# Fused SSD + latent-attention layer on one core: 64-row tiles padded, the y half of the out-projection ahead of its norm, one-bank PSUM tiles, another issue order up to the FFN

## The chip, the cores and the metric

The kernel runs on one core of a Trainium2 chip. The metric is the device time of one execution in microseconds (us), lower is better. The five engines of the core are named as the profile names them: PE (matrix multiply, with PEld for its weight loads), DVE (vector), ACT (scalar, activations), POOL (GpSimd, which also issues some DMAs) and SP (which issues most DMAs).

## The reference, cut to what matters

One layer of a hybrid encoder for 576 tokens at once, 512 of a new stream (the prompt) and 64 of a running stream (the sample), all in float32:

```
h   = rmsnorm(x, norm_mix) @ w_in            # z | xBC | dt | q latent | kv latent + rope key
xBC = silu(causal_conv(xBC))                 # 8 tiles of 128 channels
y   = ssd_scan(x, dt, A, B, C, state)        # chunked linear recurrence, 8 heads of 64
y   = rmsnorm((y + D*x) * silu(z), ssd_norm) # one factor per token, over 512 channels
o   = mla_attend(q, ckv cache + new, rope)   # 8 heads, block-causal softmax
x2  = x + concat(y, o) @ w_out               # out-projection: y half and o half
x3  = x2 + (silu(n@w_gate) * (n@w_up)) @ w_down,  n = rmsnorm(x2, norm_ffn)   # d_ff 2816
out = rmsnorm(x3, norm_final)
```

## The kernel before, in words

Everything is transposed: channels stand on the 128 partitions, the 576 tokens along the free axis, cut into 256 + 320 (`UNEVEN`) or 288 + 288 (`HC`). A float32 product is three PE products of float32r parts (high x high, high x low, low x high); DVE and ACT make those parts (`split_weights` L111/L112 for weights, `split_scaled` L143/L145 for activations). Transposes and the small products of the scan and the attention run on plain float32.

The stages, in the order of time (profiled start in brackets): the first projection (0 us), eight convolution tiles with the step sizes `dt` of the scan (from about 30 us; `in_tile`, `conv_tile`, `step_sizes`), gate tiles z and five scan chunks of 128 tokens, the fifth of 64 (`chunk_a`, `_e`, `_b`, `_s`, `gate`), the attention by four pairs of heads (`pair_proj`, `scores`, `turn`, `values`, and for the 64 sample tokens `turn_s`, `values_s`), the out-projection (`out_tile`, `last_out`), the operands of the FFN (`x_operands`), the FFN with products saved in Strassen's manner (`gu_steps`, `down_steps`, from about 262 us to 617 us), and the last norm with the sends (from L1201).

Work is first written down stage by stage by the lists `ORDER_CONV`, `ORDER_SSD`, `ORDER_ATT`, `ORDER_FFN`; then `issue_in_order` puts each engine's instructions into an order that a table of numbers per engine (`ISSUE`) spells out. So the order on each engine is fixed by hand, and each engine takes its instructions strictly in that order.

Names that the steps below use:

- `mm_tile`: a PSUM tile of two banks (`[P, 2, 512]`), from a pool of two, so four of the eight banks. `small_ps` and `bank` ("sc", "pp", "hm") give the other banks.
- `norm_y` (L172 to L179) turns the squares' sums of the gated y into the factor `Ry` per token; `cat_tile` (L764) multiplies y by `ssd_norm` and `Ry`, and `split_scaled` makes `cat_y`, the y half's operand.
- In `ORDER_ATT`, S are scores, T turns (transposes), V and W values, N is `norm_y`, y is `cat_tile`, F is the y half of an out-projection tile, X is `load_x2`. O in `ORDER_FFN` is an out tile. Before, seven tiles have an F and an O part, tile 1 is done whole in O.
- `x2` holds the residual stream. `load_x2` fetches the input x into it with two SP DMAs of 1152 KB, and the evacuations of PSUM (L750) add products to it: `x2 = ps + x2`.
- `gu_weights` (L831 to L842, L111, L112): sums and splits of the FFN's weights, `x_operands` (L815 to L822): sums and splits of the FFN's inputs; both on DVE and ACT.

## Time and profile before

| | |
|---|---|
| time of an execution, median of 3 runs | 635.18 us (634.85 to 635.65) |
| the profiled execution: its span | 633.0 us |
| what lies around the span (median of the runs less the span) | 2.2 us |
| PE busy | 622.7 us, 98% of the span |
| DVE busy | 539.3 us, 85% |
| ACT busy | 400.4 us, 63% |
| POOL busy | 117.7 us, 19% |
| chain that ended last | PE 88%, DVE 6%, ACT 2%, issue 2% |

For the profiled execution the records give its span, from the first instruction to the last; a time of its own outside the span is not recorded, so it is set against the runs' median. "Busy" of an engine is the union of its instructions' times. For PE this includes the time in which a matmul sits in the pipeline, so that a matmul that had to start late can still look busy. A bracket such as `[0.40 <-DVE sp_a L361]` at a row of the timeline says how long the engine had been idle before it and whose end let it go on.

### The profile page before, as it was taken

The page shows a single profiled execution, that of the slowest core. Times are in us where ns is not written, and L with a number is a line of the kernel's source. Part 1 is how long each engine was busy: PE and PEld are TensorE (multiplying, and loading weights), DVE is VectorE, ACT ScalarE, POOL GpSimd, SP SyncE. Part 2 cuts the span into 40 slices and gives each one's busy share as a digit, 9 for nine tenths or more (in the row PEclk, how much of TensorE's full clock was granted, in tenths as well). Part 3 has the DMA queues.
Part 4 walks back from the last instruction along what each step waited for, and adds up shares of the span by engine and source line. Part 5 has one row for each costly group of instructions (what it writes and reads, how often), then busy time and mean ns, then how long its engine had stood idle before and what let it go on. Part 6 is the DMA issues. An engine that isn't in the chain of part 4 may idle for free.

```text
span 633.0 us, 12094 instructions
## 1 busy us (share of the span) xinstructions
PE 622.7 (98%) x4635; PEld 596.3 (94%) x4635; DVE 539.3 (85%) x939; ACT 400.4 (63%) x768; POOL 117.7 (19%) x170
## 2 busy tenths in 40 slices
PE   9999999999999999999999999999999999999995
PEld 9899999986787899999999999999999999999995
DVE  6999986789776699999999888988899789976555
ACT  7655346779775567666556676566657665767364
POOL 1322104231010000001301330033104220323323
PEclk9999999999999999999999999999999999999999
DMA  8322374413231223335743986397738893689924
GB/s 320 134 61 74 95 193 127 128 61 106 77 117 34 96 72 126 89 106 178 262 128 90 221 182 152 82 193 185 169 100 162 199 202 101 100 215 251 256 41 149
DMA packets 39593, 89.19 MB, mean 141 GB/s; under 512 B 4570, under 2 KB 14312, under 8 KB 39280
## 3 DMA queue, kind: packets, MB, share of 16 engines
q1 hardware_dynamic: 26416, 63.12, 31.0%
q0 software_dynamic: 12400, 24.73, 21.3%
q8 instruction: 36, 0.59, 0.4%
q10 hardware_dynamic: 720, 0.57, 0.3%
q14 instruction: 21, 0.17, 0.1%
HBM read 62.74 MB, written 24.53 MB: 138 GB/s over the span
## 4 chain that ended last, share of the span: by engine, by line
PE 88%; DVE 6%; ACT 2%; issue 2%; POOL 1%; DMA 1%; POOLq 0%; DVEq 0%
PE ps_x L874 21%; PE ps_d L1064 14%; PE ps_z L874 10%; PE ps_in L281 7%; PE ps_y L874 5%; PE ps_o L458 4%; PE ps_z L458 4%; PE ps_first L129 3%; PE ps_d L281 2%; PE sc L672 2%; PE ps_p L874 2%; PE ps_l L281 2%; PE pv L719 1%; PE ptp L694 1%; PE ps_q L458 1%
## 5 line engine op out<-in xcount | busy, mean ns | idle before, releaser
L874 PE MATMUL ps_x<-xop,wh_gu_S 128*128 128x288 f32 x378 | 76.9, 295 | 0.0
L112 DVE TENSOR_TENSOR wl_gu_S<-gu,wh_gu_S 128x1024 fp32r<-128x1024 f32 x44 | 53.3, 1220 | 9.1 <-ACT wh_gu_S L111 6.2
L874 PEld LDWEIGHTS ps_x<-xop,wh_gu_S 128*128 128x128 f32 x378 | 60.5, 188 | 0.0
L1078 POOL DMA_DIRECT2D acc<-fz x32 | 27.9, 902 | 166.5 <-ACT fz L1075 137.8
L111 ACT CAST wh_gu_S<-gu 128x1024 fp32r<-128x1024 f32 x44 | 46.3, 1053 | 16.3 <-PE ps_y L874 8.3
L874 PE MATMUL ps_x<-xop,wl_gu_S 128*128 128x288 f32 x189 | 55.8, 295 | 0.0
L281 PE MATMUL ps_in<-xs,wh_in 128*128 128x256 f32 (+1 forms) x256 | 51.2, 296 | 0.4 <-DVE sp_a L361 0.4
L281 PEld LDWEIGHTS ps_in<-xs,wh_in 128*128 128x128 f32 x256 | 40.8, 188 | 1.2 <-issue 1.1
L281 PE MATMUL ps_in<-xs,wl_in 128*128 128x320 f32 (+1 forms) x128 | 37.7, 295 | 0.0
L874 PEld LDWEIGHTS ps_x<-xop,wl_gu_S 128*128 128x128 f32 x189 | 35.6, 188 | 0.0
L111 ACT CAST wh_gu_A<-gu 128x1024 fp32r<-128x1024 f32 x22 | 23.1, 1050 | 10.6 <-PE ps_x L874 7.2
L874 PE MATMUL ps_z<-xop,gu_a 128*128 128x288 f32 x189 | 29.5, 294 | 0.0
L458 PE MATMUL ps_o<-cat_y,wh_out 128*128 128x256 f32 (+1 forms) x128 | 28.9, 311 | 0.5 <-DVE cat_y L145 0.3
L112 DVE TENSOR_TENSOR wl_gu_A<-gu,wh_gu_A 128x1024 fp32r<-128x1024 f32 x22 | 26.8, 1218 | 1.5 <-ACT wh_gu_A L111 1.3
L1023 POOL DMA_DIRECT2D acc<-dn x8 | 4.4, 544 | 121.5 <-ACT dn L1022 121.5
L874 PE MATMUL ps_x<-xop_last,wh_gu_S 128*128 128x288 f32 x126 | 26.9, 295 | 0.0
L874 PEld LDWEIGHTS ps_z<-xop,gu_a 128*128 128x128 f32 x189 | 26.5, 188 | 0.0
L1064 PE MATMUL ps_d<-pair,d_1h 128*128 128x288 f32 x128 | 26.4, 296 | 0.0
L874 PE MATMUL ps_z<-xop,wh_gu_S 128*128 128x288 f32 x126 | 26.0, 295 | 0.0
L458 PE MATMUL ps_z<-xs,wh_z 128*128 128x256 f32 (+1 forms) x128 | 25.8, 296 | 0.1
L874 PE MATMUL ps_y<-xop,wh_gu_A 128*128 128x288 f32 x126 | 25.8, 296 | 0.0
L458 PE MATMUL ps_o<-cat_o,wh_out 128*128 128x320 f32 (+1 forms) x128 | 25.4, 294 | 0.3 <-DVE x L750 0.3
(418 smaller groups left out, 2164.1 us busy)
## 6 DMA issues: line engine op xcount, KB each, us to landing
gu<-in_w_gu SPq DMA_DIRECT2D x44, 512.0 KB, 5.3
wr_d<-in_w_down SPq DMA_DIRECT2D x18, 512.0 KB, 4.2
acc<-fz POOLq DMA_DIRECT2D x16, 288.0 KB, 7.2
acc<-da POOLq DMA_DIRECT2D x16, 288.0 KB, 8.0
acc<-dc POOLq DMA_DIRECT2D x16, 288.0 KB, 8.5
wr_in<-in_w_in SPq DMA_DIRECT2D x8, 512.0 KB, 3.8
wr_out<-in_w_out SPq DMA_DIRECT2D x8, 512.0 KB, 3.4
cumb<-cumD SPq DMA_DIRECT2D x5, 512.0 KB, 4.0
```

The costliest lines, as they stand in the source:

```text
L111: act.copy(hi, raw)
L112: dve.tensor_tensor(lo, raw, hi.bitcast(F32), ALU.subtract)
L129: pe.matmul(ps[:m, hf, : cols.stop - cols.start], w, x[:, cols], start=start and k == 0 and i == 0, stop=stop and k == last and i == 2,)
L281: pe.matmul(ps, w, x[:, cols], start=first and k == 0 and i == 0, stop=last and k == len(terms) - 1 and i == 2,)
L458: pe.matmul(ps[:, :n], w, x[:, cols], start=k == 0 and i == 0, stop=k == len(terms) - 1 and i == 2,)
L672: pe.matmul(s[:, :nk], qs[:, j, q0 : q0 + P], ks[:, j, :nk], start=True, stop=True)
L694: pe.transpose(pp[:, k : k + P], prs[p, i][:, j, b * P : b * P + P], ident)
L719: pe.matmul(pv[64 * j : 64 * j + 64, b * P :], V[b][:, h * HD : (h + 1) * HD], pts[p, b, j], start=b == 0, stop=True, skip_group_check=b > 0,)
L874: pe.matmul(ps, p, q, start=not onto and first and kp == kps[0] and j == 0, stop=onto or (last and kp == kps[-1] and j == 2), skip_group_c ...
L1023: pool.dma_start(acc[1][t], dn)
L1064: pe.matmul(ps, p, v, start=not onto and n == 0 and j == 0, stop=onto or (n == len(ks) - 1 and j == 2), skip_group_check=onto,)
L1078: pool.dma_start(out, src, accum_op=ALU.add)
```

## The change

1. **64-row tiles padded.** The last chunk of the scan takes the last 128 tokens (`window(c)`) as its rows and zeroes the step sizes of the first 64, so its transposes and contractions have 128 rows; the `dt` transposes of 24 rows become products with the identity; the fifth tile of V and the transposed sample probabilities (`pt_s`, one lasting tile with zeroed rows) have 128 rows.
2. **The y half ahead of its norm.** `cat_tile` no longer multiplies by `Ry`; the evacuation of F does (`x2 = ps * Ry`), and the input x is added to each tile by a POOL DMA that accumulates (288 KB each, eight of them) in place of the two SP DMAs. All eight y halves are F now, and O has the o half alone, so tile 1 has two evacuations more.
3. **One-bank PSUM tiles.** `mm_tile` is one bank, from a pool of four; what needs both halves takes two (`mm_pair`). The norm factor of the first projection, the rope of q and one q latent tile are worked in halves on that account.
4. **Another issue order** on all five engines up to the first out-projection tiles of the FFN stage: on PE, products, transposes and scores alternate in smaller pieces.
5. **Last factor on all partitions.** The sums of the last norm's second part are formed on all 128 partitions by products with a matrix of ones in two blocks of 128 columns, and the factor is worked on 256 columns; the sums by token, the diagonal matrix, the ten warming matmul records and the four products that spread the factor go. The gains of the last norm come from two copies (`gl0`, `gl1`).

The core of the diff:

```
-    psA_, psA = open_pool("psA", bufs=2, space=PSUM)
+    psA_, psA = open_pool("psA", bufs=4, space=PSUM)
...
     def mm_tile(name):
-        return psA.tile([P, 2, 512], F32, tag="mm", name=name)
+        return psA.tile([P, 512], F32, tag="mm", name=name)
+
+    def mm_pair(name):
+        return [mm_tile(f"{name}_{hf}") for hf in range(2)]
...
+    def window(c):
+
+        t0 = min(c * P, T - P)
+        return slice(t0, t0 + P)
...
-            n = P if c < 4 else TS
-            pe.transpose(pdt[:n, c * 24 : c * 24 + 24], k1[0:24, c * P : c * P + n], ident[:24, :24])
-        pool.memset(dt, 0.0)
+            pe.matmul(pdt[:, c * 24 : c * 24 + 24], k1[:, window(c)], ident[:, :24], start=True, stop=True)
...
     def chunk_a(c):
...
-            pe.transpose(px[:L, t * P : t * P + P], xsd[:, t, tk], ident)
+            pe.transpose(px[:, t * P : t * P + P], xsd[:, t, tw], ident)
...
     def chunk_s(c):
-            pe.matmul(pst[:, g * 256 : g * 256 + 256], bt[:L, g * P : g * P + P], xw[:L, g * 256 : g * 256 + 256], start=True, stop=True)
+            pe.matmul(pst[:, g * 256 : g * 256 + 256], bt[:, g * P : g * P + P], xw[:, g * 256 : g * 256 + 256], start=True, stop=True)
...
     def values_s(p):
-                    pv[64 * j : 64 * j + 64], V[4 + b][:kn, h * HD : (h + 1) * HD],
-                    pts[p, 4][:kn, b * P + j * TS : b * P + j * TS + TS], start=b == 0, stop=b == 2,
+                    pv[64 * j : 64 * j + 64], V[4 + b][:, h * HD : (h + 1) * HD],
+                    pt_s[:, b * P + j * TS : b * P + j * TS + TS], start=b == 0, stop=b == 2,
...
     def out_tile(hfs, t):
         def evac(ps, cols):
-            dve.tensor_tensor(x2[t][:, cols], ps, x2[t][:, cols], ALU.add)
+            y = x2[t][:, cols]
+            if hfs[0]:
+                dve.tensor_tensor(y, ps, y, ALU.add)
+            else:
+                dve.tensor_tensor(y, ps, Ry[:, cols], ALU.mult)
         product_halves(terms, UNEVEN, f"ps_o{hfs[-1]}_{t}", evac)
+        if not hfs[0]:
+            pool.dma_start(x2[t], a["xT"][:, t], accum_op=ALU.add)
...
     def cat_tile(t):
-        dve.scalar_tensor_tensor(xsd[:, t], xsd[:, t], col(C_SN + t), Ry, ALU.mult, ALU.mult)
         s = slot(ypool, "a1", f"cat_y{t}")
-        split_scaled(s, xsd[:, t], None)
+        split_scaled(s, xsd[:, t], col(C_SN + t))
...
     def load_x2():
-            sp.dma_start(z, a["xT"][:, 4 * i2 : 4 * i2 + 4])
...
     def last_out(t):
-        hfs = (1,) if t in begun else (0, 1)
+        hfs = (1,)
...
-ORDER_ATT = "q11 N S03 y0 y1 y2 ... T30 t3 F6 W3 V3"
+ORDER_ATT = "q11 N S03 y0 y1 y2 ... T30 t3 F6 F1 W3 V3"
...
-        token_sums(pn1, ss3[:, parts[1]], True, False)
-        token_sums(pn1, q[KT - 1], False, True)
-        diag = tmp("diag", W1)
...
+        y0, u = (tmp(f"nr_{z}", W1) for z in "yu")
+        act.activation(y0, pn1, AF.Ln, scale=1.0 / D)
+        act.activation(y0, y0, AF.Exp, scale=-0.5)
+        dve.tensor_tensor(u, y0, y0, ALU.mult)
+        dve.scalar_tensor_tensor(u, pn1, -0.5 / D, u, ALU.mult, ALU.mult)
+        Rs = R3[:, parts[1]]
+        dve.scalar_tensor_tensor(Rs, u, 1.5, y0, ALU.add, ALU.mult)
+        Rp = lbank("sc", "ps_r3", 1)
+        act.copy(Rp, Rs)
```

What moves, at three places. First DVE around the norm of y, before. `Ry` is the factor, L764 multiplies y by it, L145 makes the operand `cat_y` that PE waits for; `mx` and `sm` are maxima and sums of the softmax:

```order
L178 TENSOR_TENSOR nr_u<-nr_u,nr_v 128x288
L657 RECIPROCAL sm<-sm 128x2
L179 SCALAR_TENSOR_TENSOR Ry<-nr_u,nr_y 128x288
L662 TENSOR_SCALAR pr_0_2000<-pr_0_2000,sm 128x128
L764 SCALAR_TENSOR_TENSOR xsd<-xsd,par,Ry 128x576
L657 RECIPROCAL sm<-sm 128x1
L655 TENSOR_REDUCE mx<-sc_3_0_2018 128x1
L764 SCALAR_TENSOR_TENSOR xsd<-xsd,par,Ry 128x576
L662 TENSOR_SCALAR pr_4_2013<-pr_4_2013,sm 128x320
L764 SCALAR_TENSOR_TENSOR xsd<-xsd,par,Ry 128x576
L145 TENSOR_TENSOR cat_y_1955<-xsd,cat_y_1955 128x576
```

The same place on DVE after (the multiplication by `ssd_norm` now sits in L147, the second half of the split; two of the four `cat_y` splits stand further ahead):

```order
L177 TENSOR_SCALAR nr_v<-R_98 128x288
L147 SCALAR_TENSOR_TENSOR cat_y_1989<-xsd,par,cat_y_1989 128x576
L668 TENSOR_REDUCE mx<-sc_3_1_2046 128x1
L670 RECIPROCAL sm<-sm 128x1
L675 TENSOR_SCALAR pr_4_2039<-pr_4_2039,sm 128x320
L182 TENSOR_TENSOR nr_u<-nr_u,nr_v 128x288
L147 SCALAR_TENSOR_TENSOR cat_y_2058<-xsd,par,cat_y_2058 128x576
L183 SCALAR_TENSOR_TENSOR Ry<-nr_u,nr_y 128x288
L177 TENSOR_SCALAR nr_v<-R_98 128x288
L668 TENSOR_REDUCE mx<-sc_3_0_2044 128x1
L764 TENSOR_TENSOR x_0_2074<-ps_o_0_0_2138,Ry 128x256
```

All four splits come ahead of the factor, and the factor is first read at the evacuation of tile 0's y half. Second, PE at the first scores of the attention, before (`sc` are scores, `ps_q` the projection of the next pair's queries, `ps_g` the squares' sums of y):

```order
L458 MATMUL ps_q_1_1913<-cqn_480,wl_pair_1827 128x288
L458 MATMUL ps_q_1_1913<-cqn_483,wh_pair_1826 128x288 x2
L458 MATMUL ps_q_1_1913<-cqn_483,wl_pair_1827 128x288
L672 MATMUL sc_2_1_1982<-ks_382,qs_381 128x384
L587 MATMUL ps_g_1877<-ysq_1875,ones 128x128 x3
L672 MATMUL sc_0_0_1994<-ks_382,qs_381 128x128
L672 MATMUL sc_0_1_1996<-ks_382,qs_381 128x128
L678 MATMUL sc_s<-ks_382,qs_381 64x320 x2
L672 MATMUL sc_3_0_2018<-ks_384,qs_383 128x512
L672 MATMUL sc_3_1_2020<-ks_384,qs_383 128x512
L672 MATMUL sc_2_0_2060<-ks_384,qs_383 128x384
```

Behind the last query product there only score products stand (eight matmuls), with three small ones of `ps_g` among them. After, query products and squares' sums stand between the scores:

```order
L597 MATMUL ps_g_1913<-ysq_1911,ones 128x128 x3
L685 MATMUL sc_1_1_1994<-ks_393,qs_392 128x256
L468 MATMUL ps_q_1_1942<-cqn_496,wl_pair_1854 128x288
L468 MATMUL ps_q_0_1925<-cqn_496,wh_pair_1853 128x288
L685 MATMUL sc_2_0_2006<-ks_393,qs_392 128x384
L685 MATMUL sc_2_1_2008<-ks_393,qs_392 128x384
L468 MATMUL ps_q_0_1925<-cqn_496,wh_pair_1853 128x288
L597 MATMUL ps_g_1904<-ysq_1902,ones 128x128
L468 MATMUL ps_q_0_1925<-cqn_496,wl_pair_1854 128x288
L685 MATMUL sc_0_0_2020<-ks_393,qs_392 128x128
L685 MATMUL sc_0_1_2022<-ks_393,qs_392 128x128
L597 MATMUL ps_g_1904<-ysq_1902,ones 128x128 x2
```

On POOL the eight accumulating DMAs of `x2` stand behind the last DMA of `qs` and ahead of the first of the FFN, that of tile 1 last. Third, DVE from tile 1's y half (`ps_o_1_...`, `Ry`) to its o half, after (the `gu` rows are `gu_weights` of the FFN's first tile):

```order
L764 TENSOR_TENSOR x_0_2074<-ps_o_1_1_2795,Ry 128x320
L847 TENSOR_TENSOR gu_2_2909<-gu_2_2909,gu_0_2907 128x512
L846 TENSOR_TENSOR gu_3_2910<-gu_1_2908,gu_0_2907 128x512
L848 TENSOR_TENSOR gu_3_2910<-gu_0_2907,gu_2_2909 128x512
L762 TENSOR_TENSOR x_0_2074<-ps_o_0_0_2850,x_0_2074 128x256
L112 TENSOR_TENSOR wl_gu_A_2920<-gu_0_2907,wh_gu_A_2919 128x1024
L762 TENSOR_TENSOR x_0_2074<-ps_o_0_1_2864,x_0_2074 128x320
L112 TENSOR_TENSOR wl_gu_S_2924<-gu_2_2909,wh_gu_S_2923 128x1024
L762 TENSOR_TENSOR x_0_2074<-ps_o_1_0_2878,x_0_2074 128x256
```

and the same place before, where tile 1's two halves gather in one PSUM group and have one evacuation per part of the columns (`ps_o_1_0`, `ps_o_1_1`):

```order
L750 TENSOR_TENSOR x_0_2049<-ps_o_0_0_2795,x_0_2049 128x256
L833 TENSOR_TENSOR gu_2_2878<-gu_2_2878,gu_0_2876 128x512
L832 TENSOR_TENSOR gu_3_2879<-gu_1_2877,gu_0_2876 128x512
L834 TENSOR_TENSOR gu_3_2879<-gu_0_2876,gu_2_2878 128x512
L112 TENSOR_TENSOR wl_gu_A_2889<-gu_0_2876,wh_gu_A_2888 128x1024
L750 TENSOR_TENSOR x_0_2049<-ps_o_0_1_2809,x_0_2049 128x320
L842 TENSOR_TENSOR gu_a_2886<-gu_1_2877,gu_a_2886 128x512
L112 TENSOR_TENSOR wl_gu_S_2893<-gu_2_2878,wh_gu_S_2892 128x1024
L750 TENSOR_TENSOR x_0_2049<-ps_o_1_0_2823,x_0_2049 128x256
L822 TENSOR_TENSOR xop<-xv_0_2936,xop 128x288
L112 TENSOR_TENSOR wl_gu_S_2897<-gu_3_2879,wh_gu_S_2896 128x1024
L750 TENSOR_TENSOR x_0_2049<-ps_o_1_1_2849,x_0_2049 128x320
```

Tile 1's o half now adds to an `x2` that a DMA must have completed first; between the issue of that DMA, behind the evacuation L764 at the top, and the L762 of `ps_o_1_0` stand seven DVE instructions. Before, `x2` had been in place since the attention.

## The prediction

> **What bounds the kernel now.** I read the page's head and its chain first, then the busy time by stage, then the waits of PE, then what DVE and ACT do where PE waits.

> ```profile
> span 633.0 us, 12094 instructions
> PE 622.7 (98%) x4635; PEld 596.3 (94%) x4635; DVE 539.3 (85%) x939; ACT 400.4 (63%) x768; POOL 117.7 (19%) x170
> PE 88%; DVE 6%; ACT 2%; issue 2%; POOL 1%; DMA 1%; POOLq 0%; DVEq 0%
> ```

> PE is the bound: 98% busy, 88% of the chain. The change takes hardly any matmul away, so it can gain only where PE waits, or where a matmul is slower than it need be. By stage (stretch: its length, then busy time and instructions of PE, PEld, DVE, ACT, POOL, then the granted clock, the DMA share and GB/s):

> ```profile
> 5.00:118.00 113.00, 112.41 (x851) 107.92 (x851) 100.48 (x186) 62.60 (x116) 24.32 (x50) 1.00 0.46 143
> 118.00:145.00 27.00, 27.00 (x205) 23.37 (x205) 22.94 (x45) 21.13 (x52) 7.91 (x7) 1.00 0.22 74
> 145.00:165.00 20.00, 18.31 (x101) 13.25 (x100) 19.72 (x47) 16.69 (x47) 1.99 (x4) 1.00 0.32 104
> 165.00:221.00 56.00, 56.00 (x411) 44.69 (x410) 37.20 (x95) 35.95 (x99) 1.95 (x4) 1.00 0.23 75
> 221.00:262.00 41.00, 40.57 (x303) 39.80 (x303) 40.52 (x74) 29.57 (x45) 0.00 (x0) 1.00 0.25 86
> 262.00:617.00 355.00, 355.00 (x2679) 354.74 (x2679) 308.58 (x469) 225.39 (x391) 73.48 (x89) 1.00 0.67 163
> 617.00:633.00 16.00, 9.67 (x80) 9.09 (x78) 9.53 (x27) 7.01 (x19) 5.14 (x8) 0.93 0.44 148
> ```

> The FFN, 355 of the 633 us, is full and its order unchanged: nothing there. Ahead of it PE's visible idle time is 0.59 us (convolution and scan), 1.69 (first attention) and 0.43 (out-projection), 2.71 in all, and the tail has 6.33. The granted clock is 1.00 in every stage but the tail. DVE is full from 145 to 165 and from 221 to 262, and that is where this change works.

> ```profile
> 152.01 0.76 PE L678 MATMUL sc_s<-ks,qs 100*64 100x320 f32 x4 [0.23 <-ACT pr L656]
> 153.67 0.70 PE L672 MATMUL sc<-ks,qs 100*128 100x512 f32 x1 [0.90 <-ACT pr L656]
> 155.86 0.91 PE L672 MATMUL sc<-ks,qs 100*128 100x384 f32 x2 [0.21 <-ACT pr L656]
> 160.63 0.41 PE L458 MATMUL ps_o<-cat_y,wh_out 128*128 128x320 f32 x1 [0.31 <-DVE cat_y L145]
> L764 DVE SCALAR_TENSOR_TENSOR xsd<-xsd,par,Ry x4: 807/810/810, 155.3 to 159.1; 128x576 f32<-128x576 f32 x4
> 51.87 0.49 PE L281 MATMUL ps_in<-xs,wh_in 128*128 128x256 f32 x2 [0.40 <-DVE sp_a L361]
> ```

> Three of the four waits of the first attention are for the exponentials (their PSUM banks), one is for `cat_y`, which stands behind the norm on DVE. The wait at 51.87 us is a convolution tile that finds its two-bank PSUM tile not yet emptied.

> **The change part by part.**

> *The norm off the path, products between the scores.* Four L764 of 0.81 us leave DVE, 3.24 us in the stretch where it is busy 19.72 of 20. The multiplication by `ssd_norm` moves into the split at no extra instruction, and the norm's own instructions stay but PE no longer waits for them: the first reader of `Ry` is an evacuation. On PE, query products now stand between scores, so the waits for ACT have cover. The rows show 1.65 us of waits; late starts that look busy come on top. Least gain 0.3 (the `cat_y` wait alone goes, ACT's exponentials still pace the scores), most 3.24 (DVE's saved time is all on the path). I take 2.0, near the 1.69 of idle time that the stage shows. Late next are the exponentials, ACT being busy 16.69 of 20.

> *One-bank tiles.* Half a tile can be refilled when its own half is evacuated. That takes the 0.40 us at 51.87, or up to the 0.59 idle of that stage; smaller halves cost DVE six rope instructions more. Least: a loss of 0.2 if those delay an evacuation. I take 0.5 of gain. The norm factor of the first projection in halves works beside running products, which fill PE there, and costs nothing.

> *Padding.* The 64-row matmuls of the sample's values beside their 128-row neighbours (busy us, mean ns, idle before), and the `dt` transposes:

> ```profile
> L730 PE MATMUL pvs<-pts,V 128*64 128x64 f32 x32 | 2.2, 231 | 0.0
> L730 PE MATMUL pvs<-pts,V 64*64 64x64 f32 x16 | 1.3, 243 | 0.0
> 31.09 0.49 PE L346 MATMUL ps_dt<-ident,k 24*128 24x24 f32 x5
> 31.50 0.39 PE L281 MATMUL ps_in<-xs,wl_in 128*128 128x256 f32 x1
> 624.37 0.58 PE L1236 MATMUL ps_n<-ones,sq 128*128 128x1 f32 x4
> ```

> Full rows are no slower: 16 x 12 ns are 0.2 us gained, and rather more where a 64-row piece stands between 128-row ones. Against it, `dt`: five transposes take 31.50 - 31.09 = 0.41 us; as float32 products they leave two records each (as L1236, four records for two products, 0.58 us), so ten records at some 0.11 us, +0.7. The two sum to +0.5; with -0.6 as the other end (the 64-row pieces break the pipeline more than their durations say) I take 0.

> [...]

> *Finer alternation on PE.* By the two orders, changes from float32 to float32r products rise from some 33 to some 117. One such change:

> ```profile
> 132.20 0.39 PE L507 MATMUL ps_b<-bc 128*128 128x128 f32 x2
> 132.42 0.27 PE L506 MATMUL ps_b<-ident,bc 128*128 128x128 f32 x1
> 132.53 0.39 PE L507 MATMUL ps_b<-bc 128*128 128x128 f32 x2
> 132.67 0.51 PE L458 MATMUL ps_q<-cqn,wh_pair 128*128 128x288 f32 x2
> 133.02 0.29 PE L458 MATMUL ps_q<-cqn,wl_pair 128*128 128x288 f32 x1
> 133.15 0.43 PE L458 MATMUL ps_q<-cqn,wh_pair 128*128 128x288 f32 x2
> 133.42 0.29 PE L458 MATMUL ps_q<-cqn,wl_pair 128*128 128x288 f32 x1
> ```

> Two `ps_b` take 0.22 us from start to start and two `ps_q` 0.27, together 0.49; across the change (132.53 to 133.02) it is 0.49 too. So a change costs nothing here; I allow +0.1, at most 84 x 0.01 = 0.8.

> *x by accumulating DMAs.* Two SP DMAs go, eight POOL DMAs of 288 KB come. Seven have microseconds to land. The eighth is issued behind tile 1's y evacuation, and the evacuation of its o half waits for it; queued behind that on DVE are the FFN's weight splits and all further evacuations, which PE waits for. Between the two stand on DVE:

> ```profile
> 223.65 0.68 DVE L833 TENSOR_TENSOR gu<-gu,gu 128x512 f32<-128x512 f32 x1
> 224.25 0.68 DVE L832 TENSOR_TENSOR gu<-gu,gu 128x512 f32<-128x512 f32 x1
> 225.46 1.22 DVE L112 TENSOR_TENSOR wl_gu_A<-gu,wh_gu_A 128x1024 fp32r<-128x1024 f32 x1
> 226.59 0.48 DVE L750 TENSOR_TENSOR x<-ps_o,x 128x320 f32<-128x320 f32 x1
> acc<-fz POOLq DMA_DIRECT2D x16, 288.0 KB, 7.2
> acc<-dn POOLq DMA_DIRECT2D x8, 288.0 KB, 4.1
> ```

> Three `gu` sums at 0.60 from start to start, two evacuations of some 0.37, two splits at 1.13: 4.8 us of cover. A 288 KB DMA of POOL lands in 4.1 to 7.2 us, so the wait is 0 to 2.4. The FFN's DMAs of 7.2 share the queues with many others and this stage moves only 86 GB/s, so it is nearer 4.1; I take +0.4. Tile 1's two extra evacuations are 0.7 us of DVE in a stage where it has 41.00 - 40.52 = 0.48 free, but before there was idle time just ahead:

> ```profile
> 218.54 0.22 DVE L712 TENSOR_TENSOR cat_o<-pvs,cat_o 128x64 fp32r<-128x64 f32 x1 [2.43 <-ACT cat_o L711]
> ```

> In those 2.43 us tile 1's y half and earlier `gu` sums find room: +0.1, ends -0.4 and +0.7.

> *The tail.* From the last add on DVE (623.28) to the first output (627.28) are 4.00 us.

> ```profile
> 623.28 0.42 DVE L1178 TENSOR_TENSOR sum<-ps_l,sum 128x256 f32<-128x256 f32 x1 [0.55 <-PE ps_l L281]
> 623.74 0.42 ACT L1266 ACTIVATE sq<-sum 128x256 f32<-128x256 f32 x1 [0.22 <-DVE sum L1178]
> 626.19 0.29 DVE L1290 TENSOR_SCALAR diag<-ident,Rt 128x128 f32<-128x128 f32 x1
> 627.28 1.74 DVE L1192 TENSOR_TENSOR sum<-sum,ps_r 128x256 f32<-128x256 f32 x5 [0.81 <-PE ps_r L1293]
> 627.72 0.37 ACT L1294 COPY R<-ps_r 128x256 f32<-128x256 f32 x1 [1.15 <-PE ps_r L1293]
> ```

> After: two adds of 128 columns (0.29 each) and the second square (some 0.35), a product (0.35), Ln and Exp on 256 columns (0.42 each), three DVE steps (0.42 each), the copy into PSUM (0.37): 3.75, and POOL starts a step earlier. I take -0.2, ends +0.4 and -0.8.

> Sum: -2.0 - 0.5 + 0 + 0.1 + 0.4 + 0.1 - 0.2 = -2.1; a part of the 0.43 us of waits from 221 to 262 (0.2) and of late starts elsewhere that the finer order covers (0.3) makes it -2.6. Span 633.0 - 2.6 = 630.4; with the 2.2 us around it (the median 635.18 less the span), **632.6 us**.

> **The rivals.**

> *Slower: the eighth DMA.* If it lands in 7.2 us or later, or is issued late because POOL's queue is held by the `gl` copies ahead of it, DVE stands 2.4 us or more in the out-projection, where it is full, and the evacuations hold up PE. It decides from a wait of 3.0 us (the 2.6 gained and the 0.4 already charged), and of 4.3 for a loss that can be told. Only the FFN's `fz` row speaks for it. At a landing of 10 us, 5.2 us of wait: 632.6 - 0.4 + 5.2 = 637.4.

> *Same: DVE gives it back.* PE reaches the out-projection 2.5 us earlier, but DVE's 40.5 us of work there ends when it did, less the 3.24 it saved by 165 us, since from there to 221 us it is idle for 56.00 - 37.20 us anyway: then only half of the 0.5 of the convolution, and the tail, remain, 634.7. For it: DVE 40.52 of 41. Against: 2.43 us of idle time just ahead.

> *More: the busy share hides waits.* If matmuls in small pieces lost time at each start and the new order covers it, scan and attention give 3 us more than their idle rows: 629.6. For it: matmuls that start late count as busy; against: the FFN's and convolution's rows are as regular as the change row above.

> *The change does nothing in the attention:* exponentials pace it as before and the stage gives 0.3: 632.6 + 1.7 = 634.3.

> **How the numbers follow.** 0.2%, 1.27 us, is about what a measurement of this kernel can tell from no change: 633.9 and 636.45 are the bounds. Chances: forecast 0.46, more 0.20, same 0.13, nothing in the attention 0.06, slower by the DMA (or another queue held up) 0.15. Faster is the first two, 0.66; same 0.19; slower 0.15. The forecast's own range is 631.0 to 633.8. For 8 in 10 I go down to 629.0 (a little beyond the third rival) and up to 636.2 (the same cases whole, and the smaller DMA waits).

> **What would show it.** Right: from 145 to 165 us PE idle under 0.5 us and no wait for `cat_y`; no wait of PE near 51 us; the FFN's first product some 2.4 us earlier; its length 355 us as before; the first output 0.2 us nearer to the last add. Wrong: DVE idle before the L762 of tile 1 for over 2.8 us with the accumulating DMA named; PE's idle time between 221 and 262 us grown by as much as it fell before; `ps_dt` over 1.5 us.

## The result and the profile after

The changed kernel takes 639.12 us in the median (638.13 to 641.35); the kernel before, run beside it, 635.2 us (634.42 to 635.65). The ratio is 1.0069, with a 95% interval of 1.0059 to 1.008: slower by 3.9 us. The forecast was 632.6 us, between 629.0 and 636.2: wrong in sign and outside its range.

The head of the page, and the busy time by stage with the columns of the prediction's table:

```profile
span 636.9 us, 12117 instructions
...
PE 623.4 (98%) x4626; PEld 599.5 (94%) x4626; DVE 540.0 (85%) x945; ACT 400.0 (63%) x769; POOL 124.8 (20%) x181
```

```profile
5.00:118.00 113.00, 109.66 (x818) 106.05 (x819) 98.12 (x184) 60.34 (x113) 20.45 (x43) 0.98 0.41 132
118.00:145.00 27.00, 27.00 (x214) 23.97 (x214) 22.12 (x45) 20.87 (x54) 10.39 (x13) 1.00 0.35 110
145.00:165.00 20.00, 19.85 (x114) 15.01 (x111) 19.10 (x47) 17.52 (x49) 3.45 (x6) 1.00 0.18 58
...
221.00:262.00 41.00, 40.76 (x308) 38.98 (x306) 38.23 (x72) 27.84 (x43) 2.02 (x4) 1.00 0.42 131
262.00:617.00 355.00, 355.00 (x2676) 354.70 (x2676) 310.67 (x471) 224.56 (x388) 72.06 (x87) 1.00 0.66 163
617.00:637.00 20.00, 11.18 (x91) 10.63 (x89) 11.98 (x31) 9.69 (x24) 5.82 (x8) 0.84 0.34 118
```

PE is still 98% busy, so the head says nothing. The stages do. In the first attention PE's idle time fell from 1.69 us to 0.15, and in the out-projection from 0.43 to 0.24, as hoped. But from 5 to 118 us it grew from 0.59 to 3.34, and there the granted clock is 0.98 where it was 1.00. Cut finer, one stretch of 10 us holds all of it; first the row of the changed kernel, then that of the kernel before:

```profile
86.00:96.00 10.00, 6.83 (x43) 6.62 (x42) 6.79 (x14) 2.59 (x5) 0.64 (x2) 0.83 0.67 220
```

```profile
86.00:96.00 10.00, 9.88 (x76) 9.19 (x75) 9.21 (x17) 3.67 (x5) 1.44 (x3) 1.00 0.91 241
```

33 matmuls fewer in 10 us, at a mean clock of 0.83. What PE waits for after (engine, what, for whom: us in total, times, longest), and its timeline at the place:

```profile
PE ps_z L468 <- DVE qt L446: 3.2, 1, 3.2
...
PE ps_o L468 <- DVE x L762: 0.2, 1, 0.2
PE ps_z L468 <- DVE zh L478: 0.2, 1, 0.2
```

```profile
86.63 0.29 PE L129 MATMUL ps_qr<-cqn,wl_uqr 128*128 128x288 f32 x1
90.09 0.62 PE L468 MATMUL ps_z<-xs,wh_z 128*128 128x256 f32 x3 [3.17 <-DVE qt L446]
...
90.67 0.40 PE L468 MATMUL ps_z<-xs,wh_z 128*128 128x256 f32 x2
...
93.43 0.63 PE L468 MATMUL ps_z<-xs,wh_z 128*128 128x256 f32 x2
93.86 0.41 PE L468 MATMUL ps_z<-xs,wl_z 128*128 128x256 f32 x1
```

The waits for `pr`, `cat_y` and `sp_a` are gone. In their place stands one wait of 3.17 us at the first gate product, for a rope product of the queries (`qt`, L446). Behind it the same pair of matmuls that takes 0.40 us at 90.67 takes 0.63 at 93.43. Windows of 2 us give the granted clock there (the column behind the five engines):

```profile
90.00:92.00 2.00, 1.91 (x13) 1.94 (x14) 2.00 (x3) 0.00 (x0) 0.00 (x0) 0.86 0.70 141
92.00:94.00 2.00, 2.00 (x10) 2.00 (x9) 1.15 (x2) 0.79 (x2) 0.00 (x0) 0.50 0.99 355
94.00:96.00 2.00, 2.00 (x17) 2.00 (x15) 0.00 (x0) 0.00 (x0) 0.00 (x0) 0.79 1.05 372
```

So there are two losses: the stand (the time in which PE stands still), and half the clock for 3.4 us behind it. The rope is the rotation of queries and keys by their position; a convolution tap is one multiply-add of the filter. Why the wait is for a rope product shows on DVE, in the changed kernel and then in the kernel before:

```profile
82.72 0.44 DVE L445 TENSOR_TENSOR rrp<-ps_qr,cos_sin 128x288 f32<-128x288 f32 x1
83.09 0.81 DVE L415 SCALAR_TENSOR_TENSOR cacc<-up,hcw,cacc 128x579 f32<-128x579 f32 x1
83.82 0.44 DVE L445 TENSOR_TENSOR rrp<-ps_qr,cos_sin 128x288 f32<-128x288 f32 x1
...
87.11 0.45 DVE L446 TENSOR_TENSOR qt<-ps_qr,cos_sin 128x288 f32<-128x288 f32 x1
87.92 0.82 DVE L415 SCALAR_TENSOR_TENSOR cacc<-up,hcw,cacc 128x579 f32<-128x579 f32 x1 [0.36 <-ACT cacc L413]
88.66 0.45 DVE L445 TENSOR_TENSOR rrp<-ps_qr,cos_sin 128x288 f32<-128x288 f32 x1
...
89.13 0.81 DVE L446 TENSOR_TENSOR qt<-ps_qr,cos_sin 128x288 f32<-128x288 f32 x2
```

```profile
86.35 0.75 DVE L435 TENSOR_TENSOR rrp<-ps_qr,cos_sin 128x576 f32<-128x576 f32 x1
...
87.61 1.41 DVE L436 TENSOR_TENSOR qt<-ps_qr,cos_sin 128x576 f32<-128x576 f32 x2
```

The rope is now done in half-size instructions, spread between the taps of a convolution tile (L415), and its last reads of PSUM end at 89.94 (before at 89.02). That alone need not cost PE anything; the run with both remedies below bears it out. But the banks moved. In the program before, the first rope product `ps_qr0` lies in banks 2 and 3, `ps_qr1` in 0 and 1, and the first gate tile takes bank 3: that of `ps_qr0`, read for the last time by the instruction that starts at 86.35. PE went on there at 87.24, 0.14 us after that instruction ended (87.10), with reads of the other rope tile still to come until 89.02:

```profile
86.69 0.43 PE L129 MATMUL ps_qr<-cqn,wl_uqr 128*128 128x288 f32 x2
87.24 0.48 PE L458 MATMUL ps_z<-xs,wh_z 128*128 128x256 f32 x2
```

In the program after, the halves of `ps_qr0` lie in banks 2 and 0; the second is read early (82.72 and 83.82), so the first half of `ps_qr1` takes bank 0 after it, and its second half, `ps_qr1_1`, takes bank 3. The first gate tile still takes bank 3, which is now that of the piece read last of all. The first sums of the FFN's norm (`ps_n`, the mark taken below for the FFN's start; its products `ps_p` run ahead of it) start at 263.40 us where they started at 259.87.

### The profile page after: what moved, and what is told of

The parts are those of the page before. It is cut to its first block, busy times and chain, and to the rows that moved or that the text cites. A ratio compares the mean times of both kernels' runs of the same rounds, so it can differ in the third digit from the quotient of the medians.

```text
span 636.9 us, 12117 instructions
## 1 busy us (share of the span) xinstructions
PE 623.4 (98%) x4626; PEld 599.5 (94%) x4626; DVE 540.0 (85%) x945; ACT 400.0 (63%) x769; POOL 124.8 (20%) x181
## 4 chain that ended last, share of the span: by engine, by line
PE 82%; DVE 2%; ACT 1%; issue 1%; DVEq 0%; ACTq 0%
PE ps_x L888 21%; PE ps_d L1078 14%; PE ps_z L888 10%; PE ps_o L468 8%; PE ps_y L888 5%; PE ps_l L290 4%; PE ps_z L468 3%; PE sc L685 2%; PE ps_d L290 2%; PE ps_p L888 2%; PE pv L730 2%; PE ptp L707 1%; PE ps_v L616 1%; PE ps_q L468 1%; PE ps_k L468 1%
## 5 line engine op out<-in xcount | busy, mean ns | idle before, releaser
L112 DVE TENSOR_TENSOR wl_gu_S<-gu,wh_gu_S 128x1024 fp32r<-128x1024 f32 x44 | 53.5, 1222 | 9.6 <-ACT wh_gu_S L111 6.4
L290 PE MATMUL ps_in<-xs,wl_in 128*128 128x256 f32 (+1 forms) x128 | 35.5, 296 | 0.0
L468 PE MATMUL ps_o<-cat_y,wh_out 128*128 128x256 f32 (+1 forms) x128 | 32.0, 325 | 0.0
L468 PE MATMUL ps_z<-xs,wh_z 128*128 128x256 f32 (+1 forms) x128 | 28.6, 317 | 3.3 <-DVE qt L446 3.2
L112 DVE TENSOR_TENSOR wl_gu_A<-gu,wh_gu_A 128x1024 fp32r<-128x1024 f32 x22 | 26.9, 1223 | 1.2 <-ACT wh_gu_A L111 1.0
L888 PE MATMUL ps_x<-xop,wh_gu_A 128*128 128x288 f32 x126 | 25.7, 295 | 0.0
## 6 DMA issues: line engine op xcount, KB each, us to landing
acc<-fz POOLq DMA_DIRECT2D x16, 288.0 KB, 6.8
acc<-da POOLq DMA_DIRECT2D x16, 288.0 KB, 7.8
acc<-dc POOLq DMA_DIRECT2D x16, 288.0 KB, 8.4
```

The lines of the kernel that those rows point to most:

```text
L112: dve.tensor_tensor(lo, raw, hi.bitcast(F32), ALU.subtract)
L290: pe.matmul(ps, w, x[:, cols], start=first and k == 0 and i == 0, stop=last and k == len(terms) - 1 and i == 2,)
L468: pe.matmul(ps[:, :n], w, x[:, cols], start=k == 0 and i == 0, stop=k == len(terms) - 1 and i == 2,)
L888: pe.matmul(ps, p, q, start=not onto and first and kp == kps[0] and j == 0, stop=onto or (last and kp == kps[-1] and j == 2), skip_group_c ...
```

## The experiments

The theory: the first gate tile shares its bank with the last-read rope piece; PE stands, its clock falls, and together they take more than the change's other parts give. The rivals: the rope's lateness and not the bank; the new order of products; the new tail; the `dt` products.

**Other banks for the first gate tile.** One PSUM tile is skipped, so the gate halves go to banks 6 and 7, which no rope piece holds. More moves than the gate, which the expectation does not say: every later tile of banks 3 and 4 goes to 6 and 7 as well, and those of 5, 6 and 7 go to 3, 4 and 5. Which of these tiles share a bank with each other stays the same. One small DVE copy (`ncum`) moves ahead with it, so that the bank that it reads comes free.

```
+    bank("pp", "ps_skip")
     def product_halves(terms, cuts, name, evac, hfs=(0, 1)):
```

> The changed kernel with the first gate tile's two halves in PSUM banks 6 and 7, which are empty by then, in place of banks 3 and 4 (bank 3 holds the last of the four q-rope tiles, read last at 89.9 us); the one copy of cumulated sums that reads bank 7 is put earlier on DVE. Nothing else differs from the changed kernel (639.1 us). Main theory: the changed kernel loses 3.2 us where that gate product waits for the q-rope tile and about 1.8 us more because PE's granted clock falls to half for some microseconds behind the wait; both go: about 634.1 us, no PE idle time near 87 us and a granted clock of 1.00 there. Rival (the vector engine is late as a whole from there on, so the wait only moves to the next product that it feeds): 638 to 639 us, with a new wait of about 3 us behind the gate tile.

Measured: 633.9 us (633.39 to 635.82), ratio to before 0.9988 (0.9978 to 0.9997). Compared product by product with the changed kernel, PE is 3.4 us ahead at the first gate product and 4.9 us from 92 us of its own time on, to the end of the FFN. The first gate products, with no wait at them, the clock behind them, and the one wait that the list then shows from 60 to 300 us:

```profile
86.80 0.55 PE L470 MATMUL ps_z<-xs,wh_z 128*128 128x256 f32 x3
87.19 0.28 PE L470 MATMUL ps_z<-xs,wl_z 128*128 128x256 f32 x1
```

```profile
90.00:92.00 2.00, 2.00 (x19) 2.00 (x18) 2.00 (x3) 0.00 (x0) 0.00 (x0) 1.00 0.42 113
92.00:94.00 2.00, 2.00 (x17) 1.99 (x16) 2.00 (x5) 0.79 (x2) 0.00 (x0) 1.00 0.78 246
```

```profile
PE ps_o L470 <- DVE x L764: 0.2, 1, 0.2
```

Without the collision the change is a small gain: 1.2 us beside the kernel before that was timed with it (635.09 us), between 0.2 and 1.4 by the interval.

**The rope piece earlier, the bank as it is.** On DVE the last multiplication out of PSUM moves ahead of the four instructions that stood before it: a tap of the convolution (145), the copy `ncum` (106) and two rope products of the other half (154, 155).

```
 DVE order:  ... 140 158 145 154 106 155 161 178 ...   (after)
 DVE order:  ... 140 158 161 145 154 106 155 178 ...   (161 is qt<-ps_qr1_1)
```

> The changed kernel with one vector instruction moved: the last read of the q-rope tile in bank 3 stands four instructions further ahead (directly behind the other read of that tile), which should free the bank at about 87.9 us in place of 89.9. Main theory: the wait falls from 3.2 to about 1.2 us, so 637.1 us, and 635.3 us if the shorter stand no longer makes the granted clock fall. Rival (vector engine late as a whole): 638.5 us or more.

Measured: 635.83 us (635.25 to 636.83), ratio 1.0014 (1.0004 to 1.0023). The wait falls to a third:

```profile
PE ps_z L468 <- DVE qt L446: 1.1, 1, 1.1
```

The clock stays at 1.00, and PE is 1.7 us ahead at the gate and 3.2 by 92 us; 0.4 is lost again in the out-projection, where the evacuations wait. So the release of this bank is what PE waits for, and the shorter stand saves the clock as well.

**The bank alone, in the kernel before.** There the first gate half is put on a bank of `ps_qr1`; order and tile sizes stay. The turn of the small banks moves by one with it, so many later tiles change their bank too.

```
-            ps = bank("hm", f"{name}_{hf}")
+            ps = bank("sc" if name == "ps_z0" and hf == 0 else "hm", f"{name}_{hf}")
```

> The kernel before (635.1 us), with the first half of the first gate tile in bank 0 in place of bank 3: in bank 0 is the second q-rope tile, whose last read ends at 89.0 us, while the first q-rope tile (banks 2 and 3) is read by 87.1 us. Nothing else differs but the turn of three small banks. Main theory (the loss is that of the bank, not of the halved tiles or of the new order): PE stands for 1.9 us, so 637.0 us, and about 638.5 us if a stand of this length makes the granted clock fall too (1.2 us of standing did not, 3.2 did). Rival (the bank alone does nothing without the new order): 635.1 us.

Measured: 637.26 us (636.71 to 638.5), ratio 1.0039 (1.0025 to 1.0052).

```profile
89.60 0.47 PE L458 MATMUL ps_z<-xs,wh_z 128*128 128x256 f32 x2 [2.06 <-DVE qt L436]
```

A choice of banks and nothing else makes the kernel before 2 us slower. The new order of products is not needed for it. In the traced execution the clock did not fall: 1.00 in every window of 2 us from 84 to 102 us.

**The stand filled.** In the changed kernel 13 products of ones fill PE's wait; their result is unused. They write bank 7, so the copy `ncum` that reads it moves ahead on DVE, as in the version with other banks.

```
+        pw = small_ps("sc", "ps_fill")
+        for _ in range(13):
+            pe.matmul(pw[:, :P], ones, ones, start=True, stop=True)
```

> The changed kernel with 13 small products of ones into an empty PSUM bank between the last q-rope product and the first gate product, so that PE works (some 2.9 us) while the gate product waits as before. If the fall of the granted clock follows from PE standing still, the clock stays at 1.00 and the time is about 1.8 us less, 637.3 us, though the wait is not removed. If the clock falls for another reason (the weight and decay loads that come at 92 to 96 us, say), 639.1 us as before.

Measured: 638.68 us (638.22 to 638.79), ratio 1.0059 (1.0043 to 1.0076), and not the 637.3 expected; its interval overlaps that of the changed kernel, so the trace must decide. The gate starts when it did (+0.1 us, product by product), the clock stays at 1.00, and from 94 to 224 us PE is 1.4 us ahead: the share of the fallen clock. Of that 1.1 is lost at 228 us, where PE waits for an evacuation (0.9 us at most) behind a DVE sum of FFN weights that arrive later than PE now needs them:

```profile
227.13 0.69 DVE L850 TENSOR_TENSOR gu<-gu,gu 128x512 f32<-128x512 f32 x1 [1.06 <-DMA gu<-in_w_gu]
```

**How long a stand lowers the clock.** On the kernel with the late bank the last rope product is done twice (longer) or three times (longest), so the bank is held longer by one such product each time (0.66 us by the expectation, 0.79 by the stands measured below).

```
-                dve.tensor_tensor(halves(u), rr[1], g, ALU.mult)
+            for _ in range(2 if i else 1):      # 3 for the longest
+                dve.tensor_tensor(halves(u), rr[1], g, ALU.mult)
```

> The kernel before, with the first gate tile on the last-read rope bank, and the last rope product done twice: 0.66 us more of DVE between the rope's product and the bank's release, so a stand of PE of about 2.06 + 0.66 = 2.7 us. If the granted clock falls only after a stand of 3 us or so: the clock stays 1.00 and the time is 637.26 + 0.66 = 637.9. If it falls already at 2.7: some 1.5 more, 639.4, with a granted clock of 0.5 in a stretch of some 4 us behind the stand.

> As the kernel with the longer stand, but the last rope product is done three times: a stand of about 3.4 us. Theory: PE's stand of over some 3 us makes the granted clock fall to half for some 4 us behind it, as in the changed kernel, so 637.26 + 1.32 + 1.5 = 640.1, and two stretches of 2 us near 0.50. Rival: the fall in the changed kernel had another cause (its finer order of products before and behind the stand); then the clock stays 1.00 and the time is 638.6.

Measured: 639.0 us (638.62 to 639.45), ratio 1.0061 (1.0048 to 1.0075), and 640.4 us (640.28 to 640.7), ratio 1.0084 (1.007 to 1.0098). The stand and the clock behind it, first of the longer, then of the longest:

```profile
89.58 0.47 PE L459 MATMUL ps_z<-xs,wh_z 128*128 128x256 f32 x2 [2.85 <-DVE qt L437]
```

```profile
90.00:92.00 2.00, 2.00 (x13) 2.00 (x12) 1.97 (x3) 0.00 (x0) 0.00 (x0) 0.59 1.12 281
92.00:94.00 2.00, 2.00 (x12) 2.00 (x11) 1.25 (x5) 0.94 (x2) 0.00 (x0) 0.55 0.70 233
```

```profile
90.62 0.47 PE L459 MATMUL ps_z<-xs,wh_z 128*128 128x256 f32 x2 [3.64 <-DVE qt L437]
```

```profile
92.00:94.00 2.00, 2.00 (x11) 2.00 (x11) 1.97 (x4) 0.00 (x0) 0.00 (x0) 0.50 0.85 273
```

The fall came back in a kernel with the old order, so the finer order is not its cause. In these traces it comes after 2.85, 3.17 and 3.64 us and not after 1.15 or 2.06. The 3 us of both expectations were the author's estimate, between the stands of 2.06 and 3.17 us measured by then; no run shows them as a limit. Its price: the kernel with the late bank and that with the longer stand begin the gate at the same time (89.60 and 89.58) and the FFN at 262.22 and 263.85, so 1.6 us. That the longest stand came out so near its forecast is in part luck: its trace has a second fall of the clock, from 159.42 to 162.84 us in the attention, which costs some 0.6 us (an estimate: 1.4 us between the two medians, less the 0.79 of the stand) and which the theory did not have.

**Four multiplications given back.** On the kernel with other banks, four DVE multiplications as long as those that the change saved, with an unused result, one ahead of each split of `cat_y`.

```
     def norm_y():
+        for t in range(4):
+            dve.scalar_tensor_tensor(Ry, xsd[:, t], col(C_SN + t), xsd[:, t], ALU.mult, ALU.mult)
```

> The version with the first gate tile in free banks (633.9 us), with four vector instructions more, of the kind and length of the ones that the change took away (0.81 us each, on the same data, one ahead of the second half of each cat_y split; their output is overwritten by the norm's factor and not used). If the gain in the first attention came from the vector time that the change freed, 1.5 to 3.2 us more: 635.4 to 637.1 us. If it came from the query products that now stand between the scores on PE and from the norm being off PE's path: at most 0.5 us more, 633.9 to 634.4 us.

Measured: 636.87 us (636.09 to 637.6), ratio 1.0029 (1.0019 to 1.0039): 3.0 us above the kernel that it is built on, for 3.24 us of DVE. Product by product, PE loses 2.1 us of it between 145 and 165 us. The waits of before return:

```profile
PE ps_o L470 <- DVE cat_y L147: 1.2, 1, 1.2
PE sc L687 <- ACT pr L671: 0.5, 1, 0.5
```

So most of the gain in the attention is DVE's time. What the new order on PE adds to it was not tried by itself.

**`dt` by transposes again**, on the kernel with other banks.

```
-            pe.matmul(pdt[:, c * 24 : c * 24 + 24], k1[:, window(c)], ident[:, :24], start=True, stop=True)
+            pe.transpose(pdt[:, c * 24 : c * 24 + 24], k1[0:24, window(c)], ident[:24, :24])
```

> The version with the first gate tile in free banks (633.9 us), with the step sizes turned by five transposes of 24 rows and 128 columns, as before, in place of five products with the identity. If PE is full there, each record counts: the profile after shows ten dt records from 44.24 to 45.16 us, that of before five from 31.09 to 31.39, so 0.6 us less, 633.3 us. Rival (the padding pays in the pipeline what the records cost): 633.9 us.

Measured: 634.39 us (633.83 to 635.51), ratio 0.9992 (0.9983 to 1.0001): not faster. The place in the changed kernel, and here:

```profile
44.24 1.19 PE L361 MATMUL ps_dt<-ident,k 128*128 128x24 f32 x10
45.27 0.48 PE L290 MATMUL ps_in<-xs,wh_in 128*128 128x256 f32 x2
```

```profile
44.83 0.48 PE L361 MATMUL ps_dt<-ident,k 24*128 24x24 f32 x5
45.25 0.50 PE L290 MATMUL ps_in<-xs,wh_in 128*128 128x256 f32 x2
```

The products take 1.03 us from start to start and the transposes 0.42: the 0.6 us are there. Product by product 0.46 of it is gained by 44 us and 0.35 given back by 56 us.

**The old tail**, on the changed kernel and on that with other banks: token sums, diagonal and spreading products as before the change.

```
-            for b, cols in enumerate(BL if t == KT - 1 else [slice(0, W1)]):
-                y = x2[t][:, parts[1]][:, cols]
...
+        token_sums(pn1, ss3[:, parts[1]], True, False)
+        token_sums(pn1, q[KT - 1], False, True)
```

> The changed kernel with the last factor worked as before (sums by token, diagonal, product with ones; ten warming matmul records). The profiles put the end of the program 10.6 us behind the start of the last large matmul after and 10.0 before. If that is the new tail's price: about 638.5 us. If it is only the spread between executions: 639.1 us. If the new tail saves 0.2 us, as forecast: 639.3 us.

> The version with the first gate tile in free banks (633.9 us), with the last factor worked as before. The old tail on the changed kernel gave 639.8 us beside 639.1 (not clear, since the two were not timed together), while the profiles put the end 10.6 us behind the start of the last large matmul with the new tail and 10.0 with the old one. If the profiles are right: 633.4 us. If the new tail is the better one: 634.5 us. If the tails are worth the same: 633.9 us.

Measured: 639.78 us (639.55 to 640.95), ratio 1.008 (1.0065 to 1.0095), and 634.54 us (633.74 to 635.41), ratio 0.9995 (0.9986 to 1.0003). Both are 0.65 us above the kernels that they are built on, but the intervals overlap; the profiles say the opposite for the first (from the FFN's start to the end of the span 373.14 us with the old tail, 373.47 with the new) and nothing for the second (373.47 and 373.46). The first trace with the old tail also has a granted clock of 0.95 through the FFN, where the others have 1.00, so it is a poor witness. The tail is worth less than these runs can tell, and it is not the cause of the loss.

**Both remedies**, other banks and the early rope piece.

> The free banks and the early last rope product together. With the free banks PE does not wait for the rope at all, so by the theory of the shared bank the second edit finds nothing left to remove: 633.9, within 0.3 of the kernel with the free banks alone. If the rope's late end also holds up what stands behind it on DVE (the weight split of the gate product and the convolution's taps), up to 0.6 more comes: 633.3.

Measured: 634.61 us (633.49 to 634.93), ratio 0.999 (0.9981 to 0.9999). No better than other banks alone: with a free bank the rope's end holds up nothing. This version and the one with other banks alone are the only ones whose intervals lie below the kernel before, by about 0.1%.

## Why the prediction was wrong, point by point

- **One-bank tiles (-0.5): the step that failed.** Its first half was right: the wait at 51.87 us is gone. Its second half, "smaller halves cost DVE six rope instructions more. Least: a loss of 0.2 if those delay an evacuation", put the worst case at 0.2. It was 4.9 us: 3.4 by the stand and 1.5 by the clock. The size of the rope instructions was weighed, and not which tile takes the bank next and which instruction reads the bank last. The two built programs show both, and the profile before had what it takes for the price: DVE is busy 9.21 of 10 us around the rope, and takes its instructions in the order of its list (one rope piece put four places ahead shortened the wait from 3.17 to 1.15 us). The tiles take the banks in turn, and the next in turn was the one still being read.
- **Norm off the path (-2.0, ends 0.3 and 3.24):** right in mechanism and about right in size. Given back, the DVE time cost 3.0 us by the medians and 2.1 by the traces; PE's idle time in the stage is 0.15 us and `cat_y` is waited for no more.
- **Padding (0, ends +0.7 and -0.6):** `dt` went to its bad end on PE, +0.6 (1.03 us for the products, 0.42 for the transposes); yet the run with transposes is no faster: of 0.46 us gained by 44 us, 0.35 is given back by 56. The sample's values take 222 ns each (48 matmuls) where they took 231 and 243. That 64-row pieces cost more than their durations, as the end of -0.6 has it, shows in the profile before: the step from a 128-row product into them is 0.20 us (from 197.64) and that out of them to the next 128-row product 0.15 (from 197.95), where 0.10 and 0.05 are usual between 128-row products of these sizes.
- **Finer alternation (+0.1):** no price found. In the kernel with other banks a transpose (L509, 90.70 us) and the gate product behind it take 0.22 us together from start to start, in the changed kernel (L507, 98.32 us, a gate product of 320 columns) 0.26. The usual steps are 0.11 for such a transpose, 0.12 and 0.15 for the products, so 0.23 and 0.26.
- **x by accumulating DMA (+0.4):** tile 1's evacuation waits 0.2 us for it in the kernel with other banks, 0.4 in that with the early rope piece, and not at all in the changed kernel. The slower rival, the eighth DMA, did not happen.
- **Tile 1's evacuations (+0.1), tail (-0.2), rest (-0.5):** in the kernel with other banks the FFN starts 1.3 us before that of the kernel before (258.54 and 259.87), not 2.4. Counting which products are done at a given time, which is rough since some records of matmuls are missing, that kernel is 0.4 us ahead at the first gate product, about even at 144 us, some 2.4 ahead at 220 us and 1.3 at the FFN. So the first attention gives some 2.4 us, the scan loses 0.4 and the out-projection 1.1. For neither loss does a wait of PE show the cause; it is open. The second is what the rival that DVE gives the gain back foresaw, in part: DVE is busy for 40.67 of 41 us there. That DVE is the cause is not shown. In the tail the first output comes 4.16 us after the last add (4.00 before), so the -0.2 is not seen.
- **Range and chances:** "slower" had 0.15, and that on another mechanism, worth some 5 us as well. No case had a fallen clock, though the rows before show how close PE's issue stands to the rope: the gate begins at 87.24, and the last reads of the rope end 1.8 us later; the product that takes that bank waits (2.06 us in the kernel with the late bank).

## What to carry to other kernels

When tiles change size or number, list for every bank who reads it last and who writes it next, in both programs, and look at the busy engine's order between the two; a tile that only changes its bank can cost more than the whole change brings (2.1 us in the kernel before, where the change without the collision brings 1.2). A stand on a busy matrix engine is priced twice where the clock falls on account of it (here 3.4 us and 1.5). Before undoing a change that comes out slower, mend the one new wait and time it again: here that turned +3.9 us into -1.2 (-1.4 to -0.2).

## What the runs showed of the hardware

```profile
88.01:91.42 3.41, 1.33 (x11) 1.36 (x12) 3.41 (x7) 0.00 (x0) 0.00 (x0) 1.00 0.67 191
91.42:94.83 3.41, 3.41 (x16) 3.41 (x16) 1.73 (x3) 0.79 (x2) 0.00 (x0) 0.50 0.92 333
```

In three of them it falls not at once but 0.54 us (longest stand, 90.62 to 91.16), 0.80 us (longer stand, 89.58 to 90.38) and 1.33 us (changed kernel, 90.09 to 91.42) after PE goes on. In that of the old tail, whose stand lasts to 90.48 us, it falls already at 90.03. In the changed kernel and that with the longer stand it costs 1.5 to 1.6 us on top of the stand. After 1.15 and 2.06 us it stays at 1.00, and so it does when the stand is filled with unused products. The shortest stand with a fall, 2.85 us by the records, is 3.15 us from the start of the last matmul to that of the next. No stand between 2.06 and 2.85 us was tried, and one execution of each kernel was traced.

The trace of the longest stand has 0.50 once more, from 159.42 to 162.84 us; the cause is open:

```profile
159.42:162.84 3.42, 3.42 (x7) 1.43 (x7) 3.42 (x10) 2.67 (x7) 0.56 (x2) 0.50 0.91 293
```
